# Prompt attention with two key blocks turned and multiplied together, and the modulation slab placed behind a unit's value products

## The chip, the cores and the metric

The kernel runs on one core of one Trainium2 chip. A core has five engines with queues of their own: TensorE (PE, matrix products; the profile shows its weight loads apart, as PEld), VectorE (DVE), ScalarE (ACT), GpSimd (POOL) and SyncE (SP, which here only issues DMAs). The metric is the device time of one execution in microseconds, as the median of several runs; lower is better.

## The reference

One step of a decoder layer for a prompt of 512 tokens and 8 samples of 4 new tokens, which share the weights. The input passes a modulated norm, one wide projection, a convolution branch and an attention branch; these are merged, projected and added, and a gated feed-forward layer follows. The attention has three branches (compressed blocks, selected blocks, a window), each with its own softmax and a gate per head:

```python
def attend_block(q, gates, qpos, kc, vc, ks_t, vs_t, kw, vw, kwpos, slopes):
    ...
    s_c = jnp.einsum('bqgrd,bcgd->bgrqc', q, kc).astype(jnp.float32) - sl * c_dist
    p_c = jnp.where(c_valid, jax.nn.softmax(jnp.where(c_valid, s_c, NEG), axis=-1), 0.0)
    o_c = jnp.einsum('bgrqc,bcgd->bqgrd', p_c.astype(vc.dtype), vc)
    ...
    s_s = jnp.einsum('bqgrd,bgqnkd->bgrqnk', q, k_sel).astype(jnp.float32) - slopes[None, :, :, None, None, None] * s_dist[:, :, None]
    p_s = jax.nn.softmax(jnp.where(tok_valid[:, :, None], s_s, NEG), axis=(-2, -1))
    o_s = jnp.einsum('bgrqnk,bgqnkd->bqgrd', p_s.astype(v_sel.dtype), v_sel)
    ...
    s_w = jnp.einsum('bqgrd,bkgd->bgrqk', q, kw).astype(jnp.float32) - sl * w_dist
    p_w = jax.nn.softmax(jnp.where(w_valid, s_w, NEG), axis=-1)
    o_w = jnp.einsum('bgrqk,bkgd->bqgrd', p_w.astype(vw.dtype), vw)
    o = gates[..., 0:1] * o_c + gates[..., 1:2] * o_s + gates[..., 2:3] * o_w
    return o.reshape(b, nq, N_HEADS * HEAD_DIM)

def layer(x, c, conv_prev, attend, w):
    b, t = x.shape[:2]
    mod = jax.nn.silu(c) @ w['w_ada'] + w['b_ada']
    sh1, sc1, g1, sh2, sc2, g2 = jnp.split(mod[:, None, :], 6, axis=-1)
    ...
```

There are 16 heads in 4 groups (`N_KV = 4`, 4 heads each, head width 64), and the prompt is swept in 4 blocks of 128 queries. All arithmetic is in float32.

## The kernel before

The program is unrolled Python under a tile framework. The framework assigns buffers and semaphores and plans the order on each engine: the written order is the priority, but an instruction that the plan holds ready earlier is put ahead of one that waits. `issue_after` pins single instructions behind others. Each engine then executes its list strictly in order.

**The stage of the change** is prompt attention, some 190 us in the middle of the run. The loop at its end goes over 4 head groups `g` and in each over the query blocks `i` = 3, 2, 1, 0; one pair (g, i) is a *unit*. Each step of the loop does four things, written in this order: the first half of the unit (`next(u)`), one step of the convolution's output projection (`next(ocf)`), one slab of the modulation weights (`mod_slab`), and the second half of the *previous* unit (`next(prev)`). One pre-sum DMA pair (`presum`) is issued in each step too, and the next group's query and key tiles are loaded (`q_stack`, `k_stack`).

The **first half** of a unit (L1411, L1412 or L1418, L1419): for each of 4 heads, queries by keys of both full branches (selected and window; the prompt is short enough that selection keeps all blocks), over `n = 128 (i+1)` keys. DVE takes the scores out of PSUM with the distance term and the row minimum (L1424), ACT takes the exponential and the row sum (L1425), DVE scales by gate over sum (L1437).

The **second half**, after a `yield`: TensorE turns a block of 128 queries by 128 probabilities into 128 by 128 so that it can be multiplied with the values. For each of the `i+1` key blocks j and each of 2 branches, four such turns (one per head, L1452) fill one PSUM bank `ptp`, and `pev` copies the bank into an SBUF tile `PT` of a ring of four: five copies of six on ACT (L1366), the sixth on DVE (L1368). The value products (`pv_pair`, L1446) multiply the two branches' `PT` with 64 value columns each, the first branch into PSUM partitions 0 to 63 of `acc`, the second into 64 to 127, so the two occupy different halves of TensorE's columns. The products of block j are written behind the turns of block j+1. Behind the last come four products with the compressed branch's probabilities `pct` (L1462), which were turned first (`ctp`, L1442). ACT and DVE then add the halves of `acc` into `oT` (L1464, L1465). In the trace each of these float32 products appears as two instructions, each turn as one.

**The modulation** (`mod_slab`, L416): 16 products of the 9 condition vectors (padded to 32) with a slab of 1024 by 256 weights, into four column groups of 32, two instructions each: 32. ACT copies the result, and the *previous* slab's result is turned (`modq`, L427) and stored. The slab is 1 MB, loaded by SP into one of three `raw` buffers (L240). The projection `lin` (L254, L255, L256) uses the same three buffers: a `split` on ACT and DVE (L249, L250) makes the two parts of a 128-column weight, and a step is 24 matmuls of 288 or 256 columns.

PSUM has five banks `g` for projection, turns and modulation, two banks `sc` for scores, and one `acc`. TensorE's instructions in this stage have three shapes, seen in the profile's rows: 128\*128 (projection, scores, turns), 128\*64 (value products and `pct` products), 128\*32 (modulation, and `cpt`, the compressed scores at a group's start).

Behind the stage, `oT` is split into two parts, and the output projections and the feed-forward layer follow.

Of the kernel before, what the change touches and what calls it, by code (L numbers as in the profile page):

```python
# [10 lines left out]
F32 = mybir.dt.float32  # L11
# [147 lines left out]
def build(tc, a, o):  # L159
# [19 lines left out]
    def tp_ps(nm):  # L179
        return ps.tile([128, 512], F32, tag="g", bufs=5, name=nm)  # L180
# [9 lines left out]
    def nm(s):  # L190
        uid[0] += 1
        return f"{s}_{uid[0]}"
# [11 lines left out]
    ident = cst.tile([128, 128], F32, name="ident")  # L204
# [205 lines left out]
    def mod_slab(s, v=None):  # L410
        v = slab("ada", s) if v is None else v
        p = tp_ps(nm("modp"))
        for k in range(KC):
            for hh in range(2):
                j = (k % 2) * 2 + hh
                pe.matmul(p[32 * j:32 * j + 32, 0:128], lhsT=cT[:, k, :], rhs=v[:, k, hh * 128:(hh + 1) * 128], start=(k < 2), stop=(k >= 6))  # L416
        m4 = wpool.tile([128, 128], F32, tag="m4", bufs=2, name=nm("m4"))
        act.activation(m4, p[:, 0:128], AF.Copy)
        if modp:
            modp.pop()()  # L420
        modp.append(lambda: mod_fin(s, m4))
# [940 lines left out]

    def pev(out, in_):
        pcnt[0] += 1
        if pcnt[0] % 6:
            act.activation(out, in_, AF.Copy)  # L1366
        else:
            dve.tensor_copy(out, in_)  # L1368
# [28 lines left out]
    def unit(g, i, ks, qs, pc, beside=lambda r: None):  # L1397

        n = 128 * (i + 1)
        gp, gg = g // 2, g % 2  # L1400
        sums = at.tile([128, 8], F32, tag="sums", bufs=2, name=nm("sums"))
        nms = at.tile([128, 8], F32, tag="nms", bufs=2, name=nm("nms"))
        P = {}
        for r in range(4):
            hs = SLOPES[4 * g + r]
            ql = qs[:, r, 128 * i:128 * i + 128]
            kh, kl = ks
            if 2 * n <= 512:
                sp = s_ps(nm("sp"))[:, 0:2 * n]
                spv = sp.rearrange("p (b x) -> p b x", b=2)  # L1410
                pe.matmul(sp, lhsT=ql, rhs=kh[:, :, 0:n], start=True, stop=False)  # L1411
                pe.matmul(sp, lhsT=ql, rhs=kl[:, :, 0:n], start=False, stop=True)  # L1412
                sps = [spv[:, 0, :], spv[:, 1, :]]
            else:
                sps = []
                for br in range(2):
                    sp = (s_ps if br else lin_ps)(nm("sp"))
                    pe.matmul(sp[:, 0:n], lhsT=ql, rhs=kh[:, br, 0:n], start=True, stop=False)  # L1418
                    pe.matmul(sp[:, 0:n], lhsT=ql, rhs=kl[:, br, 0:n], start=False, stop=True)  # L1419
                    sps.append(sp[:, 0:n])  # L1420
            for br in range(2):
                c = br * 4 + r
                t = oT[:, br * 4 + r, :] if g == 0 and i == 3 else atp.tile([128, 512 if i % 2 else 384], F32, tag="PX" if i % 2 else "PY", bufs=8, name=nm("P"))
                p_ops.append(dve.tensor_tensor_reduce(out=t[:, 0:n], in0=sps[br], in1=t_dist[:, 512 - n:512], scale=-hs, scalar=3e38, op0=ALU.add, op1=ALU.min, accum_out=nms[:, c:c + 1]))  # L1424
                e_ops.append(act.activation(t[:, 0:n], t[:, 0:n], AF.Exp, scale=-1.0, bias=nms[:, c:c + 1], accum_out=sums[:, c:c + 1]))  # L1425
                P[br, r] = t
            beside(r)
        fac = at.tile([128, 8], F32, tag="fac", bufs=2, name=nm("fac"))
        dve.reciprocal(fac, sums)
        dve.tensor_mul(fac.rearrange("p (b r) -> p b r", b=2), fac.rearrange("p (b r) -> p b r", b=2), gtok[:, i, g * 12:(g + 1) * 12].rearrange("p (r b) -> p b r", b=3)[:, 1:3])  # L1430
        for br in range(2):
            for r in range(4):
                c = br * 4 + r
                if g == 0 and i == 3 and br:
                    act.activation(P[br, r][:, 0:n], P[br, r][:, 0:n], AF.Copy, scale=fac[:, c:c + 1])
                else:
                    dve.tensor_scalar_mul(P[br, r][:, 0:n], P[br, r][:, 0:n], fac[:, c:c + 1])  # L1437
        yield
        acc = acc_ps(nm("acc"))
        pend = None  # L1440
        tp = tp_ps(nm("ctp"))
        pe.transpose(tp[:, 0:128], pc[:, i].rearrange("p r c -> p (r c)"), ident)  # L1442
        act.activation(pct, tp[:, 0:128], AF.Copy)
        def pv_pair(j, pts_):
            for br in range(2):
                pe.matmul(acc[br * 64:br * 64 + 64, :], lhsT=vtok[br][:, j, g * 64:(g + 1) * 64], rhs=pts_[br], start=(j == 0), stop=False)  # L1446
        for j in range(i + 1):
            pts_ = []
            for br in range(2):
                tp = tp_ps(nm("ptp"))  # L1450
                for r in range(4):
                    pe.transpose(tp[:, r * 128:(r + 1) * 128], P[br, r][:, 128 * j:128 * j + 128], ident)  # L1452
                ptt = at.tile([128, 512], F32, tag="PT", bufs=4, name=nm("PT"))
                pev(ptt, tp)
                pts_.append(ptt)
            if pend is not None:
                pv_pair(*pend)
            pend = (j, pts_)
        pv_pair(*pend)
        for r in (0, 2, 1, 3):  # L1460
            q = (r // 2) * 64
            pe.matmul(acc[q:q + 64, r * 128:(r + 1) * 128], lhsT=vm[:, g, r, :], rhs=pct, start=False, stop=(r % 2 == 1))  # L1462
        tmp = at.tile([128, 512], F32, tag="PT", bufs=4, name=nm("otmp"))[0:64]
        act.activation(tmp, acc[64:128, :], AF.Copy)  # L1464
        dve.tensor_add(oT[gg * 64:gg * 64 + 64, gp * 4:gp * 4 + 4, 128 * i:128 * i + 128], acc[0:64, :].rearrange("p (r q) -> p r q", r=4), tmp.rearrange("p (r q) -> p r q", r=4))  # L1465
# [25 lines left out]
    prev = None  # L1491
    nslab = 8
    ocf = oc_gen()
    for g in range(4):
        qs, ks = qst, kst
        pc = cmp_probs(g, qs) if g else first_pc
        for i in (3, 2, 1, 0):
            u = unit(g, i, ks, qs, pc) if g or i < 3 else first_unit
            if g or i < 3:
                next(u)  # L1500
            next(ocf, None)
            mod_slab(nslab, mods_ahead.pop(0) if mods_ahead else None)
            nslab += 1
            presum(g > 0 or i < 2)
            if prev is not None:
                next(prev, None)
            prev = u
            if g < 3 and i == 3:
                qst = q_stack(g + 1)
            if g < 3 and i == 2:  # L1510
                kst = k_stack(g + 1)
    next(prev, None)
    for _ in ocf:
        pass
    modp.pop()()
    make_A(n2T, sc2, A2)
    at2st.close()
# [520 lines left out]
```

## Time and profile before

| | us |
|---|---|
| three runs | 1217.94, 1222.52, 1222.0 |
| median | 1222.0 |
| profiled execution | 1217.62 |
| its span, first to last instruction | 1215.6 |
| value products L1446, 160 instructions, busy | 44.4 |
| turns L1452, 288 instructions, busy | 36.8 |
| modulation L416, 768 instructions, busy | 27.7 |
| copies of `PT` on ACT, 67, busy | 36.3 |
| copies of `PT` on DVE, 13, busy | 8.9 |

The table's last five rows are from the profile's groups by line and shape. The 288 turns are those of `P`; the 32 of the first unit, whose probabilities lie in `oT`, are a group of their own. Of the modulation's 768 instructions only those of 16 slabs belong to this stage, the others run earlier. A matmul's duration includes its way through the array, and successive ones overlap, so busy times of PE don't add up to the time that it needs; the distance between starts is what an instruction costs in a stream. A row of the timeline names the start, the time from the first start to the last end, the engine, the line, what is written and read, the shape and the number of merged instructions.

### The profile page before, as it was taken

What the parts mean: (1) busy time and instruction counts of PE and PEld (TensorE: products, weight loads), DVE (VectorE), ACT (ScalarE), POOL (GpSimd) and SP (SyncE); (2) the same over time, 40 slices, a digit from 0 to 9 for tenths busy, and PEclk for the clock granted to TensorE, in tenths of its full rate; (3) what the DMA queues carried; (4) which work ended last, traced back from release to release, by engine and by line L of the source; (5) the groups of instructions that cost most, each with busy time, mean ns of one, the idle gap of its engine ahead of it and who ended that gap; (6) DMA issues with size and microseconds to landing.
All of it is one profiled execution on the core that took longest, in us unless ns stands there. A gap on an engine that the chain in (4) does not pass through costs nothing. (4 is left out here: it accounts for less than half of the span.)

```text
span 1215.6 us, 25753 instructions
## 1 busy us (share of the span) xinstructions
PE 1197.7 (99%) x10162; PEld 1103.2 (91%) x10162; DVE 825.7 (68%) x1891; ACT 637.5 (52%) x1292; POOL 100.2 (8%) x154
## 2 busy tenths in 40 slices
PE   9999999999999999999999999999999999999997
PEld 7999999999999888887777879999999999999996
DVE  2536656887775477686767866658746877876776
ACT  1414535654446333386766765427655666666542
POOL 1000410000000111111100100000010001001000
PEclk9999999999999999999999999999999999999999
DMA  9953266786664987979878779734466459439512
GB/s 327 407 179 140 98 193 206 212 250 199 213 208 152 373 329 291 304 219 239 256 208 245 195 216 298 221 147 168 107 179 192 149 164 265 150 132 253 200 53 74
DMA packets 82251, 255.64 MB, mean 210 GB/s; under 512 B 9032, under 2 KB 17096, under 8 KB 67930
## 3 DMA queue, kind: packets, MB, share of 16 engines
q1 hardware_dynamic: 69442, 229.85, 54.4%
q0 software_dynamic: 12112, 23.09, 11.7%
q8 instruction: 80, 1.31, 0.4%
q10 hardware_dynamic: 576, 1.05, 0.2%
q14 instruction: 41, 0.34, 0.1%
HBM read 223.15 MB, written 65.28 MB: 237 GB/s over the span
## 5 line engine op out<-in xcount | busy, mean ns | idle before, releaser
L254 PE MATMUL lin<-h_h,wh 128*128 128x288 f32 (+1 forms) x352 | 104.0, 296 | 0.6 <-ACT h_h L396 0.6
L255 PE MATMUL lin<-h_l,wh 128*128 128x288 f32 (+1 forms) x352 | 101.6, 289 | 0.0
L256 PE MATMUL lin<-h_h,wl 128*128 128x288 f32 (+1 forms) x352 | 101.0, 288 | 0.0
L303 ACT ACTIVATE work<-wA 128x272 f32<-128x272 f32 x141 | 55.4, 393 | 72.0 <-PE wA L256 70.3
L397 DVE TENSOR_TENSOR Wl<-ws,Wh 128x1024 fp32r<-128x1024 f32 (+1 forms) x47 | 55.4, 1179 | 44.9 <-ACT Wh L396 41.5
L250 DVE TENSOR_TENSOR wl<-raw,wh 128x1024 fp32r<-128x1024 f32 (+1 forms) x50 | 56.8, 1135 | 31.2 <-ACT wh L249 31.1
L249 ACT ACTIVATE wh<-raw 128x1024 fp32r<-128x1024 f32 (+1 forms) x50 | 49.2, 985 | 52.7 <-PE lin L255 33.7
L1425 ACT ACTIVATE P<-P,nms 128x384 f32<-128x384 f32 (+3 forms) x120 | 65.0, 544 | 20.1 <-DVE nms L1424 19.3
L254 PEld LDWEIGHTS lin<-h_h,wh 128*128 128x128 f32 x352 | 66.7, 190 | 8.5 <-issue 6.2
L1424 DVE CUSTOM_DVE_ANT_0 P<-sp,ta 128x384 f32<-128x384 f32 (+3 forms) x120 | 52.1, 469 | 30.2 <-PE sp L1412 22.7
L255 PEld LDWEIGHTS lin<-h_l,wh 128*128 128x128 f32 x352 | 66.3, 188 | 0.2
L256 PEld LDWEIGHTS lin<-h_h,wl 128*128 128x128 f32 x352 | 66.0, 188 | 0.1
L397 DVE TENSOR_TENSOR wl<-ws,wh 128x1024 fp32r<-128x1024 f32 (+1 forms) x47 | 55.4, 1179 | 15.5 <-ACT wh L396 14.2
L396 ACT ACTIVATE wh<-raw 128x1024 fp32r<-128x1024 f32 (+2 forms) x51 | 51.1, 1003 | 23.9 <-PE wC L255 15.7
L396 ACT ACTIVATE Wh<-ws 128x1024 fp32r<-128x1024 f32 (+1 forms) x47 | 48.0, 1022 | 29.1 <-PE wC L255 28.4
L396 ACT ACTIVATE wh<-ws 128x1024 fp32r<-128x1024 f32 (+1 forms) x47 | 48.1, 1024 | 28.4 <-PE wB L255 24.4
L660 PE MATMUL phi<-gt,wphi 128*128 128x128 f32 x512 | 61.1, 277 | 0.0
L660 PEld LDWEIGHTS phi<-gt,wphi 128*128 128x128 f32 x512 | 58.9, 193 | 1.7 <-DMA gt<-in_cache_cmp 0.8
L397 DVE TENSOR_TENSOR wl<-raw,wh 128x1024 fp32r<-128x1024 f32 (+2 forms) x51 | 58.6, 1148 | 2.4 <-ACT wh L396 2.4
L559 POOL DMA_DIRECT2D pre<-in_wt x28 | 27.2, 972 | 368.4 <-DMA pre<-in_wt 368.4
L651 DVE TENSOR_TENSOR xs<-gt 128x1024 f32<-128x1024 f32 x16 | 19.5, 1225 | 49.6 <-PE phi L660 33.5
L254 PE MATMUL wA<-S_hi,Wh 128*128 128x272 f32 x152 | 45.7, 300 | 0.1
(595 smaller groups left out, 4257.5 us busy)
## 6 DMA issues: line engine op xcount, KB each, us to landing
raw<-in_wt SPq DMA_DIRECT2D x88, 1024.0 KB, 6.5
sraw<-in_cache_sel SPq DMA_DIRECT2D x64, 256.0 KB, 4.8
gt<-in_cache_cmp SPq DMA_DIRECT2D x60, 256.0 KB, 5.8
pre<-in_wt SPq DMA_DIRECT2D x20, 512.0 KB, 9.3
pre<-in_wt POOLq DMA_DIRECT2D x20, 512.0 KB, 7.3
ws<-pre SPq DMA_DIRECT2D x20, 512.0 KB, 3.3
raw<-in_wt SPq DMA_DIRECT2D x12, 768.0 KB, 5.2
wraw<-in_cache_winT SPq DMA_DIRECT2D x8, 1024.0 KB, 8.3
```

The source lines that it names most:

```text
L249: act.activation(oh, view, AF.Copy)
L250: dve.tensor_sub(ol, view, oh.bitcast(F32))
L254: pe.matmul(p, lhsT=wh[:, k, :], rhs=xh, start=start, stop=False, **kw)
L255: pe.matmul(p, lhsT=wh[:, k, :], rhs=xl, start=False, stop=False, **kw)
L256: pe.matmul(p, lhsT=wl[:, k, :], rhs=xh, start=False, stop=stop, **kw)
L303: o_.snap_ops.append(act.activation(t, p, AF.Copy))
L396: act.activation(hi, src, AF.Copy)
L397: return dve.tensor_sub(lo, src, hi.bitcast(F32))
L559: pool.dma_start(dst, src, accum_op=ALU.add)
L660: pe.matmul(po[:, c0:c0 + 128], lhsT=w[:, ch], rhs=x[:, :, ch * 16:ch * 16 + 16], start=(n_ == 0 and ch == 0), stop=(n_ == 2 and ch == 7))
L1424: p_ops.append(dve.tensor_tensor_reduce(out=t[:, 0:n], in0=sps[br], in1=t_dist[:, 512 - n:512], scale=-hs, scalar=3e38, op0=ALU.add, op1=A ...
L1425: e_ops.append(act.activation(t[:, 0:n], t[:, 0:n], AF.Exp, scale=-1.0, bias=nms[:, c:c + 1], accum_out=sums[:, c:c + 1]))
```

## The change

In a unit's second half the key blocks are taken in groups: with four blocks (0, 1) and (2, 3), with three (0) and (1, 2), with two or one all at once. All turns of a group are written first, then all its value products. The four products with `pct` move from behind the last block to behind block 0. A unit with one block yields between its turns and its products. In the loop the previous unit's second half comes ahead of `mod_slab`, with a second `next(prev)` behind it that runs the rest of a one-block unit; the last unit gets its second `next` after the loop. `pev` gives every fourth copy to DVE. No arithmetic is added or removed, except that sums in `acc` are formed in another order.

```diff
     def pev(out, in_):
         pcnt[0] += 1
-        if pcnt[0] % 6:
+        if pcnt[0] % 4:
             act.activation(out, in_, AF.Copy)
         else:
             dve.tensor_copy(out, in_)
...
-        def pv_pair(j, pts_):
-            for br in range(2):
-                pe.matmul(acc[br * 64:br * 64 + 64, :], lhsT=vtok[br][:, j, g * 64:(g + 1) * 64], rhs=pts_[br], start=(j == 0), stop=False)
-        for j in range(i + 1):
-            pts_ = []
-            for br in range(2):
-                tp = tp_ps(nm("ptp"))
-                for r in range(4):
-                    pe.transpose(tp[:, r * 128:(r + 1) * 128], P[br, r][:, 128 * j:128 * j + 128], ident)
-                ptt = at.tile([128, 512], F32, tag="PT", bufs=4, name=nm("PT"))
-                pev(ptt, tp)
-                pts_.append(ptt)
-            if pend is not None:
-                pv_pair(*pend)
-            pend = (j, pts_)
-        pv_pair(*pend)
-        for r in (0, 2, 1, 3):
-            q = (r // 2) * 64
-            pe.matmul(acc[q:q + 64, r * 128:(r + 1) * 128], lhsT=vm[:, g, r, :], rhs=pct, start=False, stop=(r % 2 == 1))
+
+        def turn(j, br):
+            tp = tp_ps(nm("ptp"))
+            for r in range(4):
+                pe.transpose(tp[:, r * 128:(r + 1) * 128], P[br, r][:, 128 * j:128 * j + 128], ident)
+            ptt = at.tile([128, 512], F32, tag="PT", bufs=4, name=nm("PT"))
+            pev(ptt, tp)
+            return ptt
+
+        for js in ((0, 1), (2, 3)) if i == 3 else ((0,), (1, 2)) if i == 2 else (tuple(range(i + 1)),):
+            pts_ = {(j, br): turn(j, br) for j in js for br in range(2)}
+            if i == 0:
+                yield
+            for j in js:
+                for br in range(2):
+                    pe.matmul(acc[br * 64:br * 64 + 64, :], lhsT=vtok[br][:, j, g * 64:(g + 1) * 64], rhs=pts_[j, br], start=(j == 0), stop=(j == i and j > 0))
+                if j == 0:
+                    for r in (0, 2, 1, 3):
+                        q = (r // 2) * 64
+                        pe.matmul(acc[q:q + 64, r * 128:(r + 1) * 128], lhsT=vm[:, g, r, :], rhs=pct, start=False, stop=(i == 0 and r % 2 == 1))
...
             next(ocf, None)
+            if prev is not None:
+                next(prev, None)
             mod_slab(nslab, mods_ahead.pop(0) if mods_ahead else None)
+            if prev is not None:
+                next(prev, None)
             nslab += 1
             presum(g > 0 or i < 2)
-            if prev is not None:
-                next(prev, None)
             prev = u
...
     next(prev, None)
     for _ in ocf:
         pass
+    next(prev, None)
     modp.pop()()
```

More of the change, by code (lines that the diff above doesn't have):

```diff
@@ L1439, in unit @@
         acc = acc_ps(nm("acc"))
-        pend = None
         tp = tp_ps(nm("ctp"))
```

## The prediction

> **What bounds the kernel now.** I read the page first, then the stretch of the change in the table by windows, then TensorE's timeline there.
>
> ```profile
> span 1215.6 us, 25753 instructions
> PE 1197.7 (99%) x10162; PEld 1103.2 (91%) x10162; DVE 825.7 (68%) x1891; ACT 637.5 (52%) x1292; POOL 100.2 (8%) x154
> ```
>
> ```profile
> 541.60:732.70 191.10, 190.74 (x1653) 142.82 (x1652) 136.00 (x486) 128.58 (x357) 19.55 (x19) 1.00 0.82 226
> 732.70:1215.60 482.90, 471.22 (x3676) 462.28 (x3676) 343.86 (x661) 267.29 (x474) 28.92 (x35) 1.00 0.55 171
> ```
>
> The columns of the second fence are the stretch, its length, the busy time of PE, weight loads, DVE, ACT and POOL, the granted clock, the DMA share and GB/s. The first row is prompt attention after its first unit, 191.1 us, and PE shows busy for 190.74 of them. So TensorE is the bound, and DVE (136.00) and ACT (128.58) have room on average. Behind the stage PE is busy 471.22 of 482.90 with the DMA engines at 0.55, so time taken out of the stage should nearly all reach the end.
>
> The Trainium skill ("Trainium Kernel Development and Optimization", Performance Expectations) calls matmul busy time a bad measure, since matmuls overlap, and the share of weight loads a good one. By that measure the stage has room (142.82 of 191.10, against 462.28 of 482.90 behind it), where the busy column shows none. The starts of the matmuls say how much can be had.
>
> One unit in the timeline (start, us, what, count), the unit with three key blocks:
>
> ```profile
> 555.97 0.29 PE L255 MATMUL lin<-yin_lo,wh 128*128 128x288 f32 x1
> 556.10 0.29 PE L256 MATMUL lin<-yin_hi,wl 128*128 128x288 f32 x1
> 556.33 1.08 PE L416 MATMUL modp<-raw,cT 128*32 128x128 f32 x32
> 557.34 0.33 PE L427 MATMUL modq<-ident,m 128*128 128x128 f32 x1
> 557.50 0.27 PE L1442 MATMUL ctp<-ident,pc 128*128 128x128 f32 x1
> 557.61 1.91 PE L1452 MATMUL ptp<-ident,P 128*128 128x128 f32 x16
> 559.45 1.08 PE L1446 MATMUL acc<-PT,vtok 128*64 128x512 f32 x4
> 560.46 1.09 PE L1452 MATMUL ptp<-ident,P 128*128 128x128 f32 x8
> 561.48 1.94 PE L1446 MATMUL acc<-PT,vtok 128*64 128x512 f32 x8
> 563.25 0.61 PE L1462 MATMUL acc<-pct,vm 128*64 128x128 f32 x8
> 563.79 0.39 PE L1411 MATMUL sp<-kh,qs 128*128 128x256 f32 x1
> 564.01 0.28 PE L1412 MATMUL sp<-kl,qs 128*128 128x256 f32 x1
> ```
>
> No gap is marked, but time is lost where the shape changes (128*128 turns, 128*64 value products, 128*32 modulation). In a run of 16 the turns start (1.91 - 0.27) / 15 = 0.109 us apart, so 8 need 0.87; the run of 8 lasts 561.48 - 560.46 = 1.02. Lost: 0.15. Four value instructions (two pairs that run side by side) take 1.01; in the run of 8 a pair costs (1.94 - 0.61) / 3 = 0.44, so 0.13 is lost. A round trip from turns to values and back costs 0.28 to 0.30. Around the modulation, the last L256 takes 0.23 to the next start instead of 0.13 (+0.10); the 32 instructions take 1.01 where eight groups at (1.08 - 0.27) / 7 = 0.116 need 0.93 (+0.08); the turn behind them takes 0.16 instead of 0.11 (+0.05): 0.23 for two changes. From L1462 to the scores: 0.54 for eight that need four pairs of about 0.11 (+0.10), and the first score matmul takes 0.22 where the next takes 0.12 (+0.10). I take **0.15 us for each change of shape**, with ends 0.11 and 0.20.
>
> **The change, part by part.** *Fewer changes of shape.* Counting in the old order for one unit (projection, modulation, turns and values, next scores): i=3 has 8, i=2 has 6, i=1 has 4, i=0 has 4. In the new order (projection, turns and values, modulation, next scores): i=3 has turns, values, turns, values, modulation, rest, so 5; i=2 also 5; i=1 has 3; i=0, whose modulation goes between its turns and its values, still 4. That is 3 + 1 + 1 + 0 = 5 per head group, 20 in all: 20 x 0.15 = **-3.0 us** (ends -2.2 and -4.0). Entering the modulation from value products instead of from the projection is seen at the start of a head group, where 128*64 passes straight to 128*32:
>
> ```profile
> 677.06 0.72 PE L1462 MATMUL acc<-pct,vm 128*64 128x128 f32 x8
> 677.71 1.06 PE L1373 MATMUL cpt<-qs,kcd 128*32 128x512 f32 x8
> ```
>
> The last of the eight starts at 677.06 + 0.72 - 0.27 = 677.51, and cpt 0.20 later instead of 0.11: +0.09, as from the projection. So this entry is not free, and I have counted it.
>
> *Scores that cut the modulation in two.*
>
> ```profile
> 591.95 0.41 PE L416 MATMUL modp<-raw,cT 128*32 128x128 f32 x2
> ...
> 592.84 1.07 PE L416 MATMUL modp<-raw,cT 128*32 128x128 f32 x30
> ```
>
> ```profile
> 644.84 0.41 PE L416 MATMUL modp<-raw,cT 128*32 128x128 f32 x2
> ```
>
> ```profile
> 695.72 1.06 PE L416 MATMUL modp<-raw,cT 128*32 128x128 f32 x26
> ```
>
> Two late scores (L1418 and L1419, in the line left out) run inside the modulation of an i=3 step and cost two changes, 0.30. It happens three times, as the counts below 32 show. In the new order turns stand there, of the scores' own shape, so it may go (-0.9) or move among the values (0). I take half: **-0.45**.
>
> *Copies of the turned blocks.* ACT copies cost 597 ns and DVE copies 685:
>
> ```profile
> L1366 ACT ACTIVATE PT<-ptp 128x512 f32<-128x512 f32 x67 | 36.3, 597 | 16.5 <-PE ptp L1452 16.5
> L1368 DVE COPY PT<-ptp 128x512 f32<-128x512 f32 x13 | 8.9, 685 | 3.4 <-PE ptp L1452 3.4
> ```
>
> All 80 go through the counter; every fourth instead of every sixth goes to DVE, 20 for 13. The 7 x 0.6 us off ACT and 7 x 0.69 onto DVE lie beside PE. What counts is lateness, because DVE keeps its order and has long work in front:
>
> ```profile
> 594.94 2.72 DVE L1437 TENSOR_SCALAR P<-P,fac 128x384 f32<-128x384 f32 x8
> 597.58 0.68 DVE L1368 COPY PT<-ptp 128x512 f32<-128x512 f32 x1
> ```
>
> ```profile
> 598.69 1.07 PE L1446 MATMUL acc<-PT,vtok 128*64 128x512 f32 x2
> 599.70 0.33 PE L1452 MATMUL ptp<-ident,P 128*128 128x128 f32 x1
> 599.96 1.07 PE L1446 MATMUL acc<-PT,vtok 128*64 128x512 f32 x2
> ...
> 601.87 1.08 PE L1446 MATMUL acc<-PT,vtok 128*64 128x512 f32 x4
> ```
>
> The copy waited for eight scalings, so the pair was split: its halves ran one after the other with a turn between. From 598.69 to 601.87 is 3.18 where a pair and eight turns take 1.01 + 1.02: 1.15 lost. Three smaller cases, the second with the DVE rows that made it late (a 1.21 us weight split ahead of the copy):
>
> ```profile
> 611.91 1.56 PE L1446 MATMUL acc<-PT,vtok 128*64 128x512 f32 x4
> ```
>
> ```profile
> 570.97 2.01 PE L1446 MATMUL acc<-PT,vtok 128*64 128x512 f32 x7
> ...
> 573.78 0.64 PE L1373 MATMUL cpt<-qs,kcd 128*32 128x512 f32 x4
> ```
>
> ```profile
> 570.39 1.21 DVE L250 TENSOR_TENSOR wl<-raw,wh 128x1024 fp32r<-128x1024 f32 x1
> ...
> 571.61 0.68 DVE L1368 COPY PT<-ptp 128x512 f32<-128x512 f32 x1
> ```
>
> ```profile
> 726.23 2.01 PE L1446 MATMUL acc<-PT,vtok 128*64 128x512 f32 x7
> ...
> 729.04 0.33 PE L1442 MATMUL ctp<-ident,pc 128*128 128x128 f32 x1
> ```
>
> The first is 0.48 longer than the same row at 559.45; the stretches at 570.97 and 726.23 take 2.81 each where eight values and eight L1462 take 563.79 - 561.48 = 2.31, so 0.50 each. So 4 of 13 DVE copies were late, for 2.63 us. At that rate 20 cost 4.05, or +1.4. Against it: the two 0.50 cases were the last copy of an i=1 unit; there the fourth copy now falls to ACT, and the eight L1462 (0.54) stand in between. I take **+0.4**; the ends are -2.6 (none late) and +14 (all 20 late at a middle price of 0.8).
>
> *Value products right behind their own turns.* In i=2 the first block is turned and multiplied alone. Two ACT copies in a row last 1.1 us:
>
> ```profile
> 585.31 1.08 ACT L1366 ACTIVATE PT<-ptp 128x512 f32<-128x512 f32 x2
> ```
>
> Nothing in the written order covers them, so the end would be 4 x 1.1 = +4.4. But the order on PE in the trace isn't the written one (scores run inside turns and modulation wherever something waits), and the turns of blocks 1 and 2 are ready: I take 0. In i=0 the modulation (1.01) is the cover now; scores were before.
>
> *The modulation's wait and the queues.* The values of an i=0 unit now queue on PE behind a modulation that waits for its weight slab. The slab's buffer also comes free later:
>
> ```profile
> 557.47 0.33 SPq L240 DMA_DIRECT2D raw<-in_wt  x1
> ```
>
> This load was issued 0.13 after the modulation ended at 557.34: SP waited for that buffer. The load, and the pre-sum copy, gate tile and key and query loads behind it in SP's order, move later by the unit's turns and values, and the POOL accumulations with them: by less than a unit, 191.1 / 16 = 12 us.
>
> ```profile
> raw<-in_wt SPq DMA_DIRECT2D x88, 1024.0 KB, 6.5
> ```
>
> A slab lands 6.5 us after its issue; with three buffers, the one that a modulation frees is used two modulations on, about 24 us later, and that use moves too. The gate, key and query tiles have a second buffer, and the pre-sums are used behind the stage. Cost 0, ends 0 and +1.
>
> Sum: -3.0 - 0.45 + 0.4 = **-3.05 us**. The profiled execution took 1217.6 (span 1215.6), so it would become 1214.5 (span 1212.5). The median of the three runs is 1222.0, 4.4 above it, so I predict **1218.9**.
>
> **The rivals.** *The copies are in time everywhere.* All four late copies and all three cuts vanish: -3.0 - 0.9 - 2.6 = -6.5, 1215.5. For it: in the new order i=3 has one pair and eight L1462 (1.4 us) before the second pair needs its DVE copy. Against it: the scalings that delayed it last 2.72.
>
> *The modulation doesn't stand behind.* Where values wait for copies, the modulation is ready and is taken first, so only the i=3 round trips go: 8 x 0.15 = 1.2, less 0.4: -0.8, 1221.2. For it: the score matmuls run ahead in just this way.
>
> *Late DVE copies, slower.* Turns now start about 1.2 us nearer the projection's end (modulation and its turn no longer lie between), while the scalings stay where they are, so copies on DVE land in front of or among them. At 0.8 each the change loses from 8 late copies upward; 14 of 20 are 11.2 - 2.6 - 3.4 = +5.2, and 16 are +6.8, 1228.8. For it: the row at 594.94. Against it: 9 of 13 were in time.
>
> *Uncovered block 0 in i=2:* -3.05 + 4.4 = +1.3, 1223.3.
>
> *The clock.* If turns let the clock fall, each run of 16 would take 1.75 more, and 16 such runs 28 us: 1247. The granted clock is 1.00 over the stage, with runs of 16 in it, and the change makes none longer. The Trainium skill ("TensorE: Matmul & The Clock Gate", Part 4) has the rule behind this, that transposes don't count as busy in the same way; the trace shows no sign of it.
>
> **How the numbers follow.** Forecast 0.45; copies in time 0.20; modulation not behind 0.14; uncovered block 0.08; late copies 0.12; clock 0.01. A measurement can tell about 0.5%, here 6.1 us, so the borders are 1215.9 and 1228.1. Faster is the second case (0.20), slower the last two (0.13), the rest is same (0.67). From 1214 to 1224 the range holds the forecast with its ends (-4.0 for the changes), 1215.5, 1221.2 and 1223.3, and leaves out the late copies and what would go beyond -8.
>
> **What would show it.** Right: turns in runs of 16 and one pair, eight L1462, one pair in i=3; the modulation's 32 behind the values and in one piece; the stage about 3 us shorter than 191.1. Wrong: rows of two value instructions with turns between, value rows over 1.08 us for four, DVE copies behind long rows of L1437, or a shorter stage with PE gaps behind it, in particular waits for weight loads.

## The result

The changed kernel took 1229.46 us (median of 5 runs, 1229.29 to 1232.14); the kernel before, beside it, 1217.94 (1216.29 to 1222.52). The ratio is 1.0092 [1.0075, 1.011]: **slower by 11.2 us**, where 1218.9 was predicted and no change thought likeliest. The profiled execution took 1232.14, at the upper end of its runs.

### The profile after

From the page: the span and the first engine row, then from the view by windows the stage and what lies behind it, with the columns of the prediction's second fence. The stage runs from the end of the projection before it (its first row on PE is a `ctp`, or the modulation where that comes first) to the first output projection.

```profile
span 1230.4 us, 25739 instructions
...
PE 1208.1 (98%) x10162; PEld 1107.0 (90%) x10162; DVE 832.3 (68%) x1898; ACT 633.3 (51%) x1285; POOL 100.5 (8%) x154
```

```profile
541.06:744.25 203.19, 200.00 (x1655) 145.18 (x1653) 142.75 (x494) 124.35 (x349) 19.72 (x19) 1.00 0.76 207
744.25:1230.40 486.15, 472.98 (x3676) 463.91 (x3676) 343.74 (x661) 267.39 (x475) 28.96 (x35) 0.99 0.55 172
```

PE's instructions are as many as before, and the granted clock of the stage is 1.00 as before. The stage is 203.19 long instead of 191.20 (+12.0), what lies behind it 486.15 instead of 482.85 (+3.3). The two profiled executions are 14.5 us apart, more than the medians, and one piece of that is seen behind the stage: after PE had waited 1.87 us there, it was granted half its clock for 3.4 us, in which it was busy throughout: about 1.7 us lost. The profile before has no such stretch between the stage and the last microseconds.

```profile
925.82 0.40 PE L256 MATMUL dn<-f_hilo,wl 128*128 128x288 f32 x1 [1.87 <-DVE wl L250]
```

```profile
926.80:930.20 3.40, 3.40 (x18) 3.40 (x17) 0.99 (x2) 0.49 (x2) 0.86 (x1) 0.50 1.04 310
```

Inside the stage PE shows *more* busy time, 200.00 for 190.79, with the same products. Which of them got longer is seen when the same view is asked for the instructions on `acc` alone, the value and `pct` products. First the kernel before:

```profile
541.55:732.75 191.20, 51.41 (x288) 21.25 (x288) 10.21 (x15) 8.95 (x16) 1.00 0.82 226
```

The changed kernel:

```profile
541.06:744.25 203.19, 62.27 (x288) 23.82 (x288) 10.24 (x15) 8.92 (x15) 1.00 0.76 207
```

The same 288 instructions keep PE busy for 62.27 us instead of 51.41: **+10.9 of the stage's +12.0**. The rest of the stage grew by 1.1.

The timeline of the changed kernel shows how, in a unit with four key blocks (PE first, then DVE):

```profile
654.04 1.11 PE L1447 MATMUL ptp<-ident,P 128*128 128x128 f32 x8
655.08 1.46 PE L1458 MATMUL acc<-PT,vtok 128*64 128x512 f32 x4
655.99 0.66 PE L1462 MATMUL acc<-pct,vm 128*64 128x128 f32 x5
656.42 0.60 PE L1458 MATMUL acc<-PT,vtok 128*64 128x512 f32 x1
656.49 0.49 PE L1462 MATMUL acc<-pct,vm 128*64 128x128 f32 x3
656.86 0.59 PE L1458 MATMUL acc<-PT,vtok 128*64 128x512 f32 x1
657.39 0.98 PE L1447 MATMUL ptp<-ident,P 128*128 128x128 f32 x7
658.30 1.07 PE L1458 MATMUL acc<-PT,vtok 128*64 128x512 f32 x2
659.30 0.76 PE L1447 MATMUL ptp<-ident,P 128*128 128x128 f32 x5
660.00 1.94 PE L1458 MATMUL acc<-PT,vtok 128*64 128x512 f32 x8
```

```profile
654.61 2.73 DVE L1437 TENSOR_SCALAR P<-P,fac 128x384 f32<-128x384 f32 x8
657.25 0.68 DVE L1368 COPY PT<-ptp 128x512 f32<-128x512 f32 x1
```

By 655.08 the unit's first two blocks are turned (the row at 654.04 holds the last of their turns and four more). Three of their copies go to ACT, the fourth, branch 1 of the second block, to DVE, where eight scalings of the next unit stand ahead; it starts at 657.25. The order on TensorE does not wait. It takes the second block's branch 0 alone (two instructions, at 656.42 and 656.86), then seven turns, then branch 1 alone at 658.30, then the other five turns. The pair is **parted**: its halves no longer run side by side. Two instructions alone take 659.30 - 658.30 = 1.00 us, 0.86 without the 0.15 for the change of shape, as much as the four of a whole pair. So a parted pair costs 0.86, and the two changes of shape around its second half 0.30.

The Trainium skill ("TensorEngine Tiling (Array Packing)", Key Properties) says that different tiles can run matmuls in parallel; the rows agree, 0.86 for four instructions in two column halves and 0.86 for two in one.

The modulation is cut by it too (i = 1, first head group):

```profile
570.85 1.07 PE L1458 MATMUL acc<-PT,vtok 128*64 128x512 f32 x2
571.85 0.41 PE L416 MATMUL modp<-raw,cT 128*32 128x128 f32 x2
...
574.48 1.07 PE L416 MATMUL modp<-raw,cT 128*32 128x128 f32 x30
```

Counted along the whole stage, the changed kernel has 11 parted pairs where before had 1, and 94 changes of shape where before had 96. The prediction had 76. Four of the parted pairs lie in units with i = 3, four in i = 1, three in i = 0. In the units with i = 2 none is parted by this count, but halves stand among `pct` products:

```profile
558.01 1.13 PE L1458 MATMUL acc<-PT,vtok 128*64 128x512 f32 x3
558.92 0.27 PE L1462 MATMUL acc<-pct,vm 128*64 128x128 f32 x1
558.98 0.59 PE L1458 MATMUL acc<-PT,vtok 128*64 128x512 f32 x1
559.03 0.98 PE L1462 MATMUL acc<-pct,vm 128*64 128x128 f32 x7
```

From start to start, the value and `pct` products of the twelve other units take 43.3 us instead of 35.8, those of the four i = 2 units 16.9 instead of 13.8, the wait shown next included.

Besides the order, one larger wait is new. Before, SP issued this slab load at 594.29, and ACT split the weight at 603.55 without waiting:

```profile
594.29 0.38 SPq L240 DMA_DIRECT2D raw<-in_wt  x1
603.55 1.05 ACT L249 ACTIVATE wh<-raw 128x1024 fp32r<-128x1024 f32 x1
```

In the changed kernel the modulation that frees its buffer ends one second half later, and the load with it:

```profile
606.35 0.33 SPq L240 DMA_DIRECT2D raw<-in_wt  x1
615.63 1.06 ACT L249 ACTIVATE wh<-raw 128x1024 fp32r<-128x1024 f32 x1 [3.25 <-DMA raw<-in_wt]
616.59 1.55 ACT L1366 ACTIVATE PT<-ptp 128x512 f32<-128x512 f32 x3
617.23 1.07 PE L1458 MATMUL acc<-PT,vtok 128*64 128x512 f32 x2 [1.60 <-ACT PT L1366]
```

The split waits 3.25 us in ACT's queue, three copies stand behind it, and the value products wait for the copies, 1.60 on PE. Behind the stage, TensorE waits for weight splits in the first 80 us; the view of waits, before and then after:

```profile
PE lin L256 <- DVE wl L250: 1.0, 2, 0.6
```

```profile
PE lin L256 <- DVE wl L250: 2.1, 3, 0.9
```

### The profile page after: what moved, and what is told of

Read it like the earlier page. It is cut to its first block, busy times and chain, and to the rows that moved or that the text cites. A ratio compares the mean times of both kernels' runs of the same rounds, so it can differ in the third digit from the quotient of the medians.

```text
span 1230.4 us, 25739 instructions
## 1 busy us (share of the span) xinstructions
PE 1208.1 (98%) x10162; PEld 1107.0 (90%) x10162; DVE 832.3 (68%) x1898; ACT 633.3 (51%) x1285; POOL 100.5 (8%) x154
## 5 line engine op out<-in xcount | busy, mean ns | idle before, releaser
L396 ACT ACTIVATE wh<-raw 128x1024 fp32r<-128x1024 f32 (+2 forms) x51 | 51.1, 1003 | 23.9 <-PE wC L255 15.7
L1458 PE MATMUL acc<-PT,vtok 128*64 128x512 f32 x160 | 58.5, 610 | 2.4 <-ACT PT L1366 1.6
```

The lines of the kernel that those rows point to most:

```text
L396: act.activation(hi, src, AF.Copy)
```

## The experiments

Fourteen kernels were timed, each beside the kernel before on the same chip. The table gives the ratio with its interval, the difference worked out from it (ratio less 1, times 1219 us), and from each profile the changes of shape and parted pairs of the stage, its length, PE's busy time on `acc`, and the rest of the stage (length less that). A parted pair is counted where another shape stands between its halves; `pct` products between halves, as at 656.49 above, lengthen `acc` without being counted.

| kernel | ratio | us | changes | parted | stage | acc | rest |
|---|---|---|---|---|---|---|---|
| before | 1 | 0 | 96 | 1 | 191.2 | 51.4 | 139.8 |
| changed | 1.0092 [1.0075, 1.011] | +11.2 | 94 | 11 | 203.2 | 62.3 | 140.9 |
| e1 pairs forced | 1.004 [1.0022, 1.0058] | +4.9 | 89 | 0 | 197.4 | 47.5 | 149.9 |
| e2 every 6th on DVE | 1.0055 [1.0034, 1.0077] | +6.7 | 84 | 6 | 196.4 | 58.3 | 138.0 |
| e3 weight split later | 1.0075 [1.0052, 1.0098] | +9.1 | 94 | 11 | 199.6 | 60.8 | 138.7 |
| e4 slab at old place | 1.001 [0.9994, 1.0026] | +1.2 | 92 | 3 | 193.3 | 53.4 | 139.9 |
| e5 all copies on ACT | 1.0039 [1.0023, 1.0055] | +4.8 | 78 | 3 | 194.8 | 56.1 | 138.7 |
| e6 before, slab moved | 1.0095 [1.0071, 1.012] | +11.6 | 92 | 6 | 203.9 | 58.4 | 145.5 |
| e7 e4 and e5 | 0.9999 [0.9984, 1.0014] | -0.1 | 86 | 0 | 194.3 | 51.1 | 143.2 |
| e8 changed, no wait for copies | 0.9966 [0.9954, 0.9979] | -4.1 | 75 | 3 | 186.1 | 49.8 | 136.2 |
| e9 before, no wait for copies | 0.9953 [0.9937, 0.9968] | -5.7 | 94 | 0 | 187.3 | 47.5 | 139.8 |
| e10 order forced | 0.9984 [0.9973, 0.9995] | -2.0 | 72 | 0 | 188.6 | 47.0 | 141.6 |
| e11 e7, split later | 1.0015 [1.0001, 1.0029] | +1.8 | 86 | 0 | 197.7 | 53.6 | 144.1 |
| e12 e9, slab moved | 1.0061 [1.0039, 1.0082] | +7.4 | 77 | 0 | 198.2 | 47.5 | 150.7 |
| e13 e8, slab at old place | 0.9952 [0.9935, 0.997] | -5.9 | 90 | 0 | 186.6 | 46.6 | 140.0 |
| e14 e1 and e5 | 0.9999 [0.9982, 1.0016] | -0.1 | 76 | 0 | 192.8 | 47.2 | 145.7 |

### First group: which part of the change carries the loss

Theory S was that the parted pairs make the loss; the rival D, that the slab's late load makes it.

**e1**: the value products are pinned in pairs, branch 1 first.

```diff
-                for br in range(2):
-                    pe.matmul(acc[...], ..., rhs=pts_[j, br], ...)
+                first = None
+                for br in (1, 0):
+                    with tc.issue_after(first.ins) if first else ExitStack():
+                        m = pe.matmul(acc[...], ..., rhs=pts_[j, br], ...)
+                    first = first or m
```

> The changed kernel with one thing added: the value products of a block's two branches are tied together (branch 1 first, branch 0 pinned right behind it), so that neither can be placed alone. In the order on TensorE this leaves 0 split pairs (11 in the changed kernel, 1 before) and 89 changes of shape (94 and 96). Theory S (the loss is split pairs, 0.86 us each for halves that no longer run side by side, and 0.15 us for each change of shape): 11 x 0.86 + 5 x 0.15 = 10.2 us less than the changed kernel, that is within 2 us of before. Theory D (the loss is the wait for a weight slab that comes later because the modulation was moved): no better than the changed kernel, about 11 us slower than before.

It came out at +4.9, between the two. `acc` fell to 47.5, below before, so the parting is gone. But the rest of the stage rose by 9.0 over the changed kernel's. The group of value products (busy, mean ns, then the idle time before them with its releasers) shows part of where:

```profile
L1460 PE MATMUL acc<-PT,vtok 128*64 128x512 f32 x160 | 41.2, 610 | 3.3 <-DVE PT L1368 1.8 <-DVE modT L431 1.1
```

The pairs now wait, in part for DVE's copies (1.8 us); turns wait another 2.7, and the modulation lies in 25 pieces instead of 19. The order had parted the pairs to fill their wait; without that filling, a part of it stands open.

**e2**: `pcnt[0] % 4` back to `% 6`.

> The changed kernel with every sixth copy on DVE again instead of every fourth. 6 split pairs and 84 changes of shape in the order on TensorE. Theory S: 5 x 0.86 + 10 x 0.15 = 5.8 us less than the changed kernel, about 5.5 us slower than before. Theory D: as the changed kernel, about 11 us slower than before.

+6.7, near S: 6 parted pairs instead of 11. The changed share of DVE's copies carries some 4.5 of the 11.2 us.

**e3**: the first weight split of an output slab is pinned behind the exponentials, out of the way of the copies.

```diff
-                wh, wl = split(so[:, :, kk * 128:(kk + 1) * 128])
+                with tc.issue_after(e_ops[-9].ins) if k2 and kk == 0 else ExitStack():
+                    wh, wl = split(so[:, :, kk * 128:(kk + 1) * 128])
```

> The changed kernel with the split of each new projection slab on ACT pinned behind the last exponential of the step before, so that no copy of a turned block stands behind a split that waits for its slab. Order on TensorE unchanged: 11 split pairs, 94 changes of shape. Theory S: only the wait of 2 to 3 us near 616 goes, so still 8 to 9 us slower than before. Theory D: within 2 us of before.

+9.1, as S said. D falls as the main cause: the stage's slab waits were worth some 2 us, though the two intervals overlap.

**e4**: blocks two at a time as in the change, but the slab stands ahead of the second half again.

```diff
-            if prev is not None:
-                next(prev, None)
             mod_slab(nslab, ...)
             if prev is not None:
                 next(prev, None)
+                next(prev, None)
```

> The changed kernel with the old place of the modulation (ahead of the previous unit's second half); grouping of blocks and every fourth copy on DVE stay. 3 split pairs and 92 changes of shape. Theory S alone: 8 x 0.86 + 2 x 0.15 = 7.2 us less than the changed kernel, about 4 us slower than before; with theory D for the rest (the slab wait goes as well): about 1 us slower than before. Theory D alone: as before.

+1.2, with three parted pairs: what was expected of S with the slab wait gone; D alone (as before) lies inside the interval too, but e3 speaks against it. So **the slab's new place carries 10.0 of the 11.2 us**; turning two blocks at a time costs about nothing by itself, and wins nothing.

### Second group: copies, and the move alone

**e5**: every copy on ACT (`% 1000`).

> The changed kernel, with all 80 copies of turned blocks on ScalarE and none on VectorE; the modulation stays behind the value products. Theory S (what counts is how often the order on TensorE parts the two value products that run side by side, 0.57 us for a half row of two and 0.30 for two more changes of tile shape): by its order it has 78 changes of shape and 3 parted places, against 96 and 1 before and 94 and 11 in the changed kernel, so 18 x 0.15 = -2.7 and 2 x 0.86 = +1.7: -1.0 us against before, and up to +2 where the later slab makes ScalarE's weight split wait. Theory C (what counts is that copies are late, and ScalarE has 20 more of 0.60 us, 12 us, in a stage where the value products wait for it already): at the changed kernel's +11 or above. Theory D (the slab that is loaded later costs most): +8 or more, since the slab is unchanged.

+4.8: C's +11 and D's +8 fell, and S's -1 to +2 missed by 3. Three pairs are parted, yet `acc` is 56.1: in several units halves stand among `pct` products, which S did not count. (The 0.57 us in the expectation is not the price that the rows above give; its sum uses 0.86.)

**e6**: the kernel before with the slab's move only.

```diff
-            mod_slab(nslab, ...)
-            nslab += 1
-            presum(g > 0 or i < 2)
             if prev is not None:
                 next(prev, None)
+            mod_slab(nslab, ...)
+            nslab += 1
+            presum(g > 0 or i < 2)
```

> The kernel before, with one edit: the modulation slab stands behind the next step of the earlier head group instead of ahead of it. Blocks are still turned and multiplied one at a time, every 6th copy on VectorE. By its order it has 92 changes of tile shape and 6 parted pairs. S: 4 x 0.15 = -0.6 and 5 x 0.86 = +4.3, so about +3.7 us against before, and some 1 to 3 more for the later slab load: +4 to +7. D alone, with no parted pairs: +1 to +3. If the move of the slab costs nothing by itself, as the prediction had it: 0.

+11.6, as much as the whole change, and more than any theory gave. The products on `acc` are only half of it (`acc` +7.0, rest +5.7). PE is idle for 6.4 us of the stage, where before it was for 0.4, most of it before value products. In the view of waits, then in PE's timeline of e6:

```profile
PE acc L1446 <- ACT PT L1366: 3.9, 3, 2.6
```

```profile
666.38 1.91 PE L1452 MATMUL ptp<-ident,P 128*128 128x128 f32 x16
670.86 1.77 PE L1446 MATMUL acc<-PT,vtok 128*64 128x512 f32 x4 [2.57 <-ACT PT L1366]
672.56 1.97 PE L1452 MATMUL ptp<-ident,P 128*128 128x128 f32 x8
```

Sixteen turns, then 2.57 us of waiting for copies: the same cost in its open form, where there was nothing to fill with. Behind this wait the granted clock is 0.50 from 672.1 to 675.5, about 1.7 us more.

**e7**: e4 with all copies on ACT.

> The changed kernel's turns and value products (two blocks at a time), with all copies on ScalarE and the slab at its old place ahead of the step. By its order it has 86 changes of tile shape and no parted pair. S: 10 x 0.15 = -1.5 and -0.86 for the one parted place that before has: -2.4 us against before, some 0.2%; no slab wait. C: ScalarE's 80 copies make value products wait, +4 or more.

-0.1. No pair is parted, but neither S's -2.4 nor C's +4 came. Here, with the slab at its old place, one weight split waits 4.50 us for its slab, and the value products behind it 2.93:

```profile
706.28 1.06 ACT L249 ACTIVATE wh<-raw 128x1024 fp32r<-128x1024 f32 x1 [4.50 <-DMA raw<-in_wt]
707.24 2.04 ACT L1366 ACTIVATE PT<-ptp 128x512 f32<-128x512 f32 x4
...
707.87 0.19 PEld L1458 LDWEIGHTS acc<-PT,vtok 128*64 128x64 f32 x2 [2.93 <-ACT PT L1366]
```

### Third and fourth group: without the wait for copies

**e8** and **e9**: in the changed kernel and in the kernel before, the value products multiply a fixed part of the value tile, pinned behind the turns that they stood behind. The turned probabilities do not reach the output; with no reader, the `PT` buffers also come free at once, so the two runs take out the wait in both directions, and the order is planned anew.

```diff
+                    with tc.issue_after(last[0].ins):
-                    pe.matmul(acc[...], ..., rhs=pts_[j, br], ...)
+                        pe.matmul(acc[...], ..., rhs=vtok[br][:, 0:2, :], ...)
```

> The changed kernel, its value products behind the turns of their group as before, but multiplying a fixed part of the value tile in place of the turned block: they wait for no copy (the copies are still made; the turned probabilities do not reach the output). Modulation and its slab as in the changed kernel. By its order: 75 changes of tile shape and 3 parted pairs. Theory K (the loss is the copies: a value product that stands close behind its own turns either waits for them or is parted from its partner while the order fills that wait): 21 x 0.15 = -3.2 and 2 x 0.86 = +1.7, -1.5 us against before, and some 11 below the changed kernel. Theory Q (the later place of the modulation and its slab load costs by itself): +7 or more, as the move alone did in e6.

> The kernel before with the same edit: value products multiply a fixed part of the value tile and wait for no copy. By its order: 94 changes of tile shape, no parted pair. K: the copies of before are covered by the next block's turns, so little is won: 2 x 0.15 and 0.86, -1.2 us, and no more than -3 with the small waits that it has. If the wait for copies were a large cost of any version: -5 or more. The difference of e8 and this one is the change without its copies: K about -0.3 to -2, Q +7 or more.

e8 is 15.3 us below the changed kernel, e9 5.7 below before. **Waiting for copies costs the old order 5.7 us and the new one 15.3.** Without it the two kernels are 1.6 apart, and their intervals overlap. K had both directions and sized the gains too small, by 2.6 and 4.5 us; e9's -5.7 is what its expectation gave for the case that the wait is a large cost in any version. For the difference K gave -0.3 to -2, and Q +7. e8's order has 75 changes of shape, the prediction's 76 but for one: in its order, e8 is the kernel that the prediction described.

**e13**: e8 with the slab at its old place.

> e8 (two blocks at a time, value products waiting for no copy) with the slab back at its old place ahead of the step. With the copies in force that move was worth 10.0 us of the changed kernel's 11.2 (e4). By its order 90 changes of tile shape against e8's 75, no parted pair against 3. Theory K2 (in the two-block kernel the move costs only through the copies that it leaves uncovered): within 2 us of e8, on either side (15 x 0.15 = +2.3 and 3 x -0.86 = -2.6), so -2.5 to -6 against before. Theory Q2 (the move costs by itself, as in e12, where it cost 13 without copies): 5 or more below e8, -9 against before.

-5.9, within 2 of e8, as K2 said. In the changed kernel the move costs 10.0 us with the wait for copies and 1.7 without, where the intervals overlap. Its stage is as long as e8's (186.6 and 186.1). What is left lies behind the stage, 486.4 in e8 and 482.0 in e13: 2.3 us of waits for weight splits in e8's first 80 us there, none in e13's, and 1.7 for a stretch at half clock (780.0 to 783.4) that e13 doesn't have. All profiles agree on this: behind the stage the ten kernels with the slab moved take 483.7 to 487.1 us, or 483.1 to 485.3 with 1.7 taken off for each 3.4 us at half clock, and the six with the slab at its old place 480.8 to 482.9.

**e12**: e9 with e6's move, the same question for the kernel before.

> e9 (the kernel before, value products multiplying a fixed part of the value tile, so that they wait for no copy) with e6's move: the modulation slab behind the next step of the earlier head group. With the copies in force that move cost 11.6 us (e6). By its order 77 changes of tile shape against e9's 94, no parted pair in either. Theory K (the move takes the cover of the copies away, and that is its whole cost): 17 x 0.15 = -2.6 us against e9, so about -8 against before. Theory Q (the place of the slab, its load or the modulation's own wait costs by itself): +3 or more against e9, so -3 against before or slower. Between them, at e9's time: both act.

+7.4, 13 above e9: **K falls here**: without the wait for copies the move costs the kernel before as much as with it, and Q's number is right. `acc` stays at 47.5 and the rest grows by 10.9. In its timeline (DVE and PE):

```profile
640.68 0.34 PE L1419 MATMUL sp<-kl,qs 128*128 128x384 f32 x1
...
641.34 3.26 DVE L1437 TENSOR_SCALAR P<-P,fac 128x512 f32<-128x512 f32 x8
...
642.10 0.34 PE L1419 MATMUL sp<-kl,qs 128*128 128x384 f32 x1
644.63 0.68 DVE L1466 TENSOR_TENSOR oT<-acc,otmp 64x512 f32<-64x512 f32 x1
...
646.05 0.39 PE L254 MATMUL lin<-yin_hi,wh 128*128 128x256 f32 x1 [3.62 <-DVE nms L1424]
```

The next unit's scores fill their banks by 642.1, DVE has eight scalings of 3.26 in front, and the projection waits 3.62 us for a bank. In e9 the same eight scalings (636.29 to 639.55) lie beside scores and projection products that have their banks. This kind of stall comes in three head groups (2.19, 3.62 and 3.40 us), and one wait of 2.43 before turns, behind a weight split that waits for its slab, is added. The view of waits has them:

```profile
PE lin L254 <- DVE nms L1424: 5.8, 2, 3.6
PE lin L254 <- DVE modT L432: 3.4, 1, 3.4
PE ptp L1453 <- ACT pct L1443: 2.4, 1, 2.4
```

Right behind the two longest of them the granted clock is 0.50 for 3.4 us each (from 646.6 and from 701.2), 1.7 us more each time. Waits and clock are 15.0 us together; 17 changes of shape fewer, at 0.15, take 2.6 off, and the stage's +10.9 is met within 1.5. e6 has none of these stalls: there PE waits 1.2 us before the projection in the whole stage. So the 13 us of e12 belong to the order that is planned once the copies are out of the way, and this run does not tell how much of e6's 11.6 the copies are. The changed kernel does not show such stalls either.

### Forcing the order

**e10**: e1 and e5 and e3 together, and the modulation's products pinned behind the last value product, in one piece.

```diff
+                with tc.issue_after(mod_behind[0].ins) if mod_behind[0] else ExitStack():
-                pe.matmul(p[...], lhsT=cT[:, k, :], ...)
+                    m = pe.matmul(p[...], lhsT=cT[:, k, :], ...)
...
                     first = first or m
+                    mod_behind[0] = m
```

> The changed kernel with its order forced: value products always in pairs (branch 1, branch 0), the modulation's 32 products in one piece behind the last value product, all copies on ScalarE, and the weight split of a new output slab behind the exponentials. By its order 72 changes of shape and no parted pair. Theory S (only the order counts): -3.6 - 0.9 = -4.5 us against before. Theory K: the pairs now wait for their copies where the order has nothing between; e1 lost about 10 us of its stage in such places and so ended at +5; here 6 fewer pieces of modulation and no slab wait, so +2 to +6.

-2.0 [0.9973, 0.9995]: of the kernels that leave nothing out, the only one below before, by little. S's -4.5 and K's +2 to +6 both missed, on either side: `acc` is 47.0, 4.4 below before, and the rest of the stage, where pairs wait for copies, takes 1.8 of it back.

**e14**: e10 without the pinned modulation and the moved split.

> e10 without two of its edits: the modulation's products go where the order has them (19 pieces, 76 changes of tile shape) and the slab's weight split stays where it was; value products in pairs and all copies on ScalarE as in e10. e1 (pairs, every 4th copy on VectorE, 25 pieces of modulation) came out at +5, e10 at -2. If VectorE's late copies were what e1 lost: near e10, -2 to 0. If the modulation in one piece was what e10 won: near e1, +3 to +5.

-0.1: from e1 to here 5 us came from the copies on ACT, and 2 more in e10 from the other two edits. One of e14's stalls is the slab wait again:

```profile
612.39 1.06 ACT L249 ACTIVATE wh<-raw 128x1024 fp32r<-128x1024 f32 x1 [2.59 <-DMA raw<-in_wt]
613.35 1.55 ACT L1366 ACTIVATE PT<-ptp 128x512 f32<-128x512 f32 x3
```

**e11**: e7 with e3's pin.

> e7 (blocks two at a time, all copies on ScalarE, slab at its old place) with one more edit: the weight split of a new output slab stands behind the exponentials in ScalarE's queue. In e7's profile one such split waited 4.5 us for its slab, copies queued behind it, and value products lost 2.7 to 2.9 us; 86 changes of shape, no parted pair. D (that wait is the whole of what e7 lacks): 2.9 less than e7, -2.5 us against before. If the wait is one execution's accident or comes again elsewhere: as e7, 0.

+1.8. The pin did not reach the split that it was meant for; the same wait stands in the profile (4.68 us at 707.89, 4.50 in e7), value products wait 2.88 behind it, and a stretch of 3.4 us at half clock follows (from 710.6), which e7's profile doesn't have behind its wait of 2.70. So D's price for e7 was not tested.

## Why the prediction was wrong

Four steps failed, and they have one root. The prediction noted that the order on PE is not the written one and that something runs wherever a product would wait, and counted that filling as free. It is not: it parts the pair. What the prediction named as signs of being wrong is what the trace shows: rows of two value instructions with turns between, value rows over 1.08 us for four, and DVE copies behind long rows of L1437.

- **Fewer changes of shape, -3.0.** The price of 0.15 stands in the new rows (five turns in 0.70 at 659.30, 0.55 of them turns). The count failed: 2 fewer instead of 20. Of the round trips that the change removes, each parted pair puts two changes back: 96 - 20 + 10 x 2 = 96, and 94 were counted. Without the wait for copies the count is right (75 in e8).
- **Copies, +0.4.** The term mis-sized most, and the step on which the forecast failed. It carried the old rate over, 4 late of 13, at 0.66 each. But the rate belongs to the old distance between turns and products, in which the next block's turns, the modulation and the scores stood; the change takes that away. Measured, waiting for copies costs 15.3 us instead of 5.7: +9.6 in the place of +0.4, most of the 11.2.
- **Value products behind their own turns, 0.** "The turns of blocks 1 and 2 are ready" was true, and in these units no pair is parted. Yet their value and `pct` products grew by 3.1 us (16.9 for 13.8), 1.9 of it waits in one unit. In the other units the turns that were ready did the harm: standing between the halves (657.39 above), they were the mechanism of the loss, not the cover.
- **The modulation's wait and the queues, 0, at most +1.** The slab's place decided 10.0 us (e4), nearly all through the copies. By itself it cost 1.7 (e13 against e8, not clear of noise), and behind the stage the profiles are some 2 us longer in every kernel that has the move: beyond the end given. That the load moves later was seen; the weight split that waits for it, with copies queued behind, was not followed.
- **Scores cutting the modulation, -0.45.** The cuts changed their kind, not their number: 19 pieces for 18. A miss, small.

The rival of the late copies (0.12) had a right cause, though not the whole: DVE's copies behind the scalings. With all copies on ACT 4.8 of the 11.2 us are still there (e5). It took them at 0.8 each with pairs whole or split as before, and 16 late gave +6.8 over before's execution; the real form is 10 more parted pairs, at up to 0.86 and two changes of shape each, and `pct` products between halves. The range ended at 1224 because that rival was left out of it. The clock of the stage stayed at 1.00, so the rival of the clock did not come: runs of 16 turns without a wait kept it, and the stretches at half clock inside the stages of e6, e11 and e12 each follow a wait of PE. The changed kernel's stretch lies behind its stage. The step "time taken out of the stage should nearly all reach the end" held with the sign turned: all of the stage's 12.0 reached the end. Two small readings were off and changed nothing: 20 late copies at 0.8 are +13.4 rather than +14, and the load at 557.47 came 0.06 after the end of the modulation's row (556.33 + 1.08).

What stays open: how much of e6's 11.6 is its copies. Of the 3.3 us behind the changed kernel's stage 1.7 is the stretch at half clock and 1.1 more waiting for weight splits; what made the rest is not known. And a wait of PE was not always followed by half a clock (2.70 in e7 and 2.43 in e12 were not), so no run here says when it is.

## What to carry to other kernels

When products run side by side in two halves of TensorE, their price depends on both operands being ready together; where one comes by a slower route, ask what the order puts between them, since filling the wait can cost as much as the wait. Before work is moved off a place, ask which latency it covers there: here a modulation of 1.0 us, moved behind one unit's turns and values with nothing added, cost 10. And a rate of late copies read from one order says nothing of the next; the distance between producer and consumer in the new order has to be counted.

## What was not expected of the hardware

The busy time of an engine can rise by 10 us with the same instructions at the same clock: half a pair of value products holds TensorE for as long (0.86 us) as the whole pair. And a wait of PE can cost more than its length: in e6, e11 and e12 waits of 2.57 to 3.62 us were followed by 3.4 us at a granted clock of 0.50, 1.7 us more.
